# Second layer's down projection by seven products in place of eight

## The chip, the cores and the metric

The kernel runs on one core of a Trainium2 chip. Its engines are TensorE (PE in the profile, with its weight loads as PEld), VectorE (DVE), ScalarE (ACT), GpSimd (POOL) and SyncE (SP, which here issues nearly all DMAs). Each works through its own queue of instructions in order; semaphores order them among each other. On-chip memory is SBUF; PE writes its results to PSUM; DMAs move data between SBUF and the chip's DRAM. The metric is the device time of one execution in microseconds (us), lower is better.

## The reference

One inference step of a two-layer encoder for two request groups: a prompt of 1024 tokens and 8 samples of 16 tokens, 1152 tokens in all, width 1024. Layer 0 mixes tokens with RWKV-7, layer 1 with banded attention, and each ends in a SwiGLU feed-forward with adaptive norms. What matters here is the feed-forward of layer 1 (D_FF = 2816 = 22 x 128):

```python
def swiglu(h, w_gate, w_up, w_down):
    return (jax.nn.silu(h @ w_gate) * (h @ w_up)) @ w_down
...
        h = modulate(rms_norm(x, p['norm_ffn'][l]), sh_f, sc_f)
        x = x + gt_f[:, None, :] * swiglu(h, p['w_gate'][l], p['w_up'][l], p['w_down'][l])
```

All of it is float32. `x + gt_f * ...` is done in the method `residual`: one gate for all prompt tokens, one for each sample.

## The kernel before

**Layout.** Features lie on the 128 partitions, tokens along the free axis. The 1152 tokens are two column groups: c = 0 with 512 prompt tokens, c = 1 with 512 prompt and 128 sample tokens. Each group has two halves, 256 + 256 and 320 + 320.

**Precision.** A float32 product is made of three matmuls (`mm3`, line 143 issues each): both operands are split into a high part `hi` (rounded by ACT, line 272) and the rest `lo` (DVE subtracts, line 273), and hi x hi, hi x lo, lo x hi are added up in PSUM.

**Gate stage** (`gate_up`, called once per 128 rows f of D_FF, 22 of them for a layer). The two matrices `w_gate` and `w_up` are already combined by Winograd's form of Strassen's scheme: seven products instead of eight, each of 4 k x 3 passes x 2 column groups = 24 matmuls. `strassen_weights` loads four raw weight tiles (`rq`, five buffers), makes the combinations on POOL (lines 1340 to 1343) and splits them into the buffers `w`, 16 of them, two per product. The activation's seven combinations are held for the whole stage in the pools h0 and h1 (`slot`, 14 slots for each c). `gate_up` moves the products out of PSUM with ACT and DVE, adds on DVE and POOL (line 1369) and multiplies (lines 1383, 1385) into two tiles s0 and s1, the two token halves. They go to DRAM, to `sd`, by four stores. The first block, f = 0, runs in two calls, one for each c.

**Down stage** (`ffn` from the definition of `begin` on). D_FF is taken in 11 pairs p of two blocks. For each (p, c) the activations come back from `sd`, are split, and for each of the 8 output blocks n the product of this pair is added to an accumulator in SBUF (ACT copies for p = 0, line 1434; DVE adds, line 1436). For c = 0 a matmul has 512 columns, for c = 1 two matmuls have 320 each. For p = 7 the residual is added to the accumulator; for p = 8 to 10 `residual` multiplies by the gate and adds (line 1170, and lines 1174 and 1175 for the samples), and after p = 10 the block is stored.

PSUM tiles of this stage are three (`wide`: one of tag PT, two of tag S), used in turn. Temporary tiles of the gate stage (`ev("t")`) share eleven buffers.

**Order.** The program is written with a tile framework: it derives waits from the tiles, gives buffers out of pools, and orders the instructions of each engine with a simulation of times at build. Within an engine the order is then fixed. `tc.issue_after(ins)` puts what is traced in its block behind `ins` on that engine.

## Time and profile before

| | us |
|---|---|
| median of 3 runs (lowest, highest) | 3810.54 (3801.19, 3811.68) |
| the profiled execution | 3804.49 |
| its span | 3802.7 |
| second layer's down stage, first to last matmul (3520.20 to 3798.80) | 278.6 |
| from there to the end of the span | 3.9 |

The profiled execution lasts 1.8 us longer than the span, which runs from the first recorded instruction to the last. How to read the rows: a group of instructions is written as line, engine, operation, tile written <- tiles read, shape, count, then busy us, mean ns of one, and the engine's idle time just before with what ended it. A row of the timeline has the start, the length, the engine, the line, and in brackets an idle time before it. A row of the chain of waits has the start, the length and what ran. In the table of windows each stretch has the busy time of every engine; PEclk is the share of full speed that the clock was granted.

### The profile page before, as it was taken

Reading aid. Unit: us, or ns where it says so; the run is one execution under the profiler, and the core shown is the slowest. Engines: PE = TensorE matmul, PEld = TensorE weight load, DVE = VectorE, ACT = ScalarE, POOL = GpSimd, SP = SyncE. Lnnn points to the kernel's source line nnn. Section 1 sums busy time; section 2 is a strip of 40 time slices with the busy share of each in tenths; the row PEclk is TensorE's granted clock in tenths of the full one; section 3 lists DMA queues with packets and bytes.
Section 4 is the critical chain, followed back from the end, with each engine's and each line's share of the span. In section 5 each row is a group of like instructions: output and inputs, shape, how many; then the busy total and the mean of one; then the engine's idle time right before and its main releaser. Section 6 shows DMA issues by size and latency. Waiting matters only on the chain.

```text
span 3802.7 us, 72100 instructions
## 1 busy us (share of the span) xinstructions
PE 3506.1 (92%) x28550; PEld 3098.0 (81%) x28550; DVE 2263.6 (60%) x4396; ACT 1573.8 (41%) x3006; POOL 591.6 (16%) x497
## 2 busy tenths in 40 slices
PE   5889989989999799999999899789889799999999
PEld 4777778777667699999888879667677799999898
DVE  4666667765445854554457742666565755545667
ACT  5545546544223533333311452556554533333310
POOL 0000000000011154453000100000000255444000
PEclk9887899899699899999999999899899899999999
DMA  5876776776665322224654122554565322222521
GB/s 212 236 216 170 207 220 184 201 203 201 192 197 176 113 84 76 76 73 157 221 177 172 64 71 92 153 151 155 152 203 178 120 78 71 76 75 96 171 86 66
DMA packets 426995, 554.01 MB, mean 146 GB/s; under 512 B 128385, under 2 KB 292737, under 8 KB 422177
## 3 DMA queue, kind: packets, MB, share of 16 engines
q1 hardware_dynamic: 351344, 450.68, 36.9%
q0 software_dynamic: 22224, 80.36, 6.9%
q10 hardware_dynamic: 53088, 18.36, 2.1%
q8 instruction: 225, 3.69, 0.4%
q14 instruction: 114, 0.93, 0.1%
HBM read 415.85 MB, written 133.40 MB: 144 GB/s over the span
## 4 chain that ended last, share of the span: by engine, by line
PE 69%; DMA 11%; DVE 10%; issue 4%; ACT 4%; SPq 1%; ACTq 0%; POOL 0%; DVEq 0%; POOLq 0%
PE S L143 32%; PE PT L143 15%; PE acc L143 12%; PE st L143 3%; PE O L143 2%; PE G L143 1%; DVE h L273 1%; PE aux L143 1%; PE PT L1811 1%; PE Y L143 1%; DMA TT<-Z 1%; DMA h<-out_kT 1%; DVE wlo L273 1%; DMA raw<-in_rw_o 1%; DMA h<-in_wo 1%
## 5 line engine op out<-in xcount | busy, mean ns | idle before, releaser
L143 PE MATMUL S<-h,w 128*128 128x320 f32 (+1 forms) x4944 | 689.7, 298 | 12.3 <-ACT h L272 4.8
L143 PEld LDWEIGHTS S<-h,w 128*128 128x128 f32 x4944 | 671.8, 191 | 18.4 <-ACT h L272 5.6
L143 PE MATMUL S<-h,wh 128*128 128x320 f32 (+1 forms) x2844 | 529.8, 338 | 15.9 <-DVE h L1170 6.8
L143 PE MATMUL acc<-mx,whi 128*128 128x384 f32 x1728 | 508.5, 372 | 32.7 <-ACT whi L272 13.0
L143 PEld LDWEIGHTS S<-h,wh 128*128 128x128 f32 x2844 | 456.1, 189 | 70.8 <-issue 12.3
L272 ACT ACTIVATE w<-rq 128x512 fp32r<-128x512 f32 x308 | 192.6, 629 | 515.1 <-PE S L143 201.1
L143 PEld LDWEIGHTS acc<-mx,whi 128*128 128x128 f32 x1728 | 337.6, 204 | 63.3 <-ACT whi L272 16.9
L273 DVE TENSOR_TENSOR w<-rq,w 128x512 fp32r<-128x512 f32 x308 | 267.8, 872 | 199.8 <-ACT w L272 199.0
L143 PE MATMUL PT<-h,w 128*128 128x320 f32 (+1 forms) x2448 | 347.6, 297 | 10.2 <-ACT h L272 4.7
L143 PEld LDWEIGHTS PT<-h,w 128*128 128x128 f32 x2448 | 332.1, 190 | 12.2 <-ACT h L272 5.1
L143 PE MATMUL acc<-mx,wlo 128*128 128x384 f32 x864 | 316.1, 366 | 8.3 <-DVE wlo L273 8.3
L1369 POOL TENSOR_TENSOR t<-t,t 128x576 f32<-128x576 f32 (+1 forms) x132 | 226.5, 1717 | 442.2 <-ACT t L1376 320.1
L143 PE MATMUL PT<-h,wh 128*128 128x320 f32 (+1 forms) x1428 | 284.2, 342 | 8.2 <-ACT h L1558 2.3
L143 PEld LDWEIGHTS PT<-h,wh 128*128 128x128 f32 x1428 | 231.7, 188 | 38.5 <-issue 5.0
L143 PEld LDWEIGHTS acc<-mx,wlo 128*128 128x128 f32 x864 | 175.0, 203 | 20.6 <-DVE wlo L273 12.9
L273 DVE TENSOR_TENSOR wlo<-raw,whi 128x1024 fp32r<-128x1024 f32 x114 | 139.1, 1221 | 84.9 <-ACT whi L272 83.8
L272 ACT ACTIVATE wh<-rq 128x512 fp32r<-128x512 f32 x124 | 74.8, 625 | 245.1 <-PE S L143 161.4
L273 DVE TENSOR_TENSOR h<-h,h 128x1024 fp32r<-128x1024 f32 (+4 forms) x112 | 122.3, 1106 | 88.3 <-ACT h L272 72.1
L272 ACT ACTIVATE whi<-raw 128x1024 fp32r<-128x1024 f32 x114 | 119.6, 1053 | 129.0 <-PE acc L143 62.6
L272 ACT ACTIVATE h<-h 128x1024 fp32r<-128x1024 f32 (+4 forms) x112 | 103.5, 935 | 159.8 <-DMA h<-sd 111.1
L1369 DVE TENSOR_TENSOR t<-S,t 128x576 f32<-128x576 f32 (+1 forms) x116 | 86.4, 744 | 122.7 <-PE S L143 122.7
L1436 DVE TENSOR_TENSOR h<-h,S 128x640 f32<-128x640 f32 (+1 forms) x150 | 111.9, 750 | 78.9 <-PE S L143 78.7
(444 smaller groups left out, 5625.0 us busy)
## 6 DMA issues: line engine op xcount, KB each, us to landing
h<-in_wada SPq DMA_DIRECT2D x64, 512.0 KB, 6.3
rq<-in_wg SPq DMA_DIRECT2D x88, 256.0 KB, 2.6
rq<-in_wu SPq DMA_DIRECT2D x88, 256.0 KB, 2.6
rq<-in_wd SPq DMA_DIRECT2D x88, 256.0 KB, 3.1
raw<-in_wada POOLq DMA_DIRECT2D x32, 512.0 KB, 5.0
kc<-in_ck SPq DMA_DIRECT2D x16, 1024.0 KB, 5.1
vc<-in_cv SPq DMA_DIRECT2D x16, 1024.0 KB, 6.0
sd<-t SPq DMA_DIRECT2D x88, 160.0 KB, 1.9
```

What stands on the lines that cost most here:

```text
L143: return nc.tensor.matmul(out, lhsT, rhs, start=start, stop=stop)
L272: self.nc.scalar.activation(hi, x, AF.Copy)
L273: self.nc.vector.tensor_tensor(lo, x, hi, ALU.subtract)
L1369: eng.tensor_tensor(out, x, y, ALU.add)
L1436: nc.vector.tensor_tensor(y, y, d, ALU.add)
L1811: nc.tensor.transpose(pt[:, j * 128:(j + 1) * 128], P[:, j * 128:(j + 1) * 128], self.C("ident"))
```

## The change

The down projection of the second layer is computed by the same kind of seven products. Its three dimensions are halved: D_FF into even and odd blocks f, the 1024 outputs into two halves h of four blocks m, the tokens of each group into their two halves.

- The host stores `w_down[1]` as `wd1`, four quarter matrices side by side in 128 x 4 x 5632.
- During the gate stage of layer 1 `down_sums` makes the four combinations of the weights, in 32 groups g of 176 columns: a load into `ws` (two buffers), four POOL adds behind the last addition of the gate call (`last_add`), a store to the DRAM tiles `Ws`. One or two groups follow each of the calls f = 1 to 21.
- `down_open` returns what takes the place of the four stores: after an even f one block goes to DRAM and its two halves are held; after the odd f that follows, four DVE operations make the combinations and twelve stores write the other six blocks. They are stored by product and column group, as `Bd[c][i]`, each in three tiles of 4, 4 and 3 blocks. The first even block, done in two calls, takes a way through DRAM.
- `down` runs the seven products in the order 0, 1, 2, 4, 5, 6, 3. Each loads and splits its operand (6 loads, 11 k) and, for each of the four m, three pieces of weights, and issues 11 k x 3 passes x 2 column groups. Products 0, 2 and 4 are copied to SBUF and kept (`T`); the others are added to what is kept, and products 1, 5, 6 and 3 finish one quarter of the outputs each: residual and store.
- The buffers `w` are 14 instead of 16 in the second layer.

The first layer's feed-forward keeps the old loop. The diff, cut:

```diff
     for l in range(2):
         d[f"wg{l}"] = _tiles(i["w_gate"][l])
         d[f"wu{l}"] = _tiles(i["w_up"][l])
-        d[f"wd{l}"] = i["w_down"][l].reshape(22, 128, 1024)
+    d["wd0"] = i["w_down"][0].reshape(22, 128, 1024)
+    d["wd1"] = i["w_down"][1].reshape(11, 2, 128, 2, 4, 128).transpose(2, 3, 1, 4, 0, 5).reshape(128, 4, 5632)
     return {k: np.ascontiguousarray(v) for k, v in d.items()}
...
     def wq_open(self, ctx, name):
         self.wq = ctx.enter_context(self.tc.tile_pool(name="wq" + name, bufs=1, reuse_waits="tile"))
-        self.hw = ("w", "w", 16)
+        self.hw = ("w", "w", 14 if name == "1" else 16)
         self.halfraw = lambda: self.wq.tile([128, 512], F32, tag="rq", name=self.nm("rq"), bufs=5)

     def wide_open(self, ctx, name):
...
         yield put(a21)
         yield put(a22)

-    def gate_up(self, sd, B, W, cs):
+    def gate_up(self, put, B, W, cs):

         nc = self.nc
         dve = nc.vector
...
             return t[:, n0:n1]

         def add(eng, out, x, y):
-            eng.tensor_tensor(out, x, y, ALU.add)
+            return eng.tensor_tensor(out, x, y, ALU.add)

         t1, s0, s1, t5, u2, u3 = (new() for _ in range(6))
         nc.scalar.activation(t1, product(0), AF.Copy)
...
         add(gp, s1, s1, u2)
         self.silu = nc.scalar.activation(s1, s1, AF.Silu)
         add(dve, u3, product(6), u2)
-        add(gp, t5, t5, u3)
+        self.last_add = add(gp, t5, t5, u3)
         dve.tensor_tensor(s1, s1, t5, ALU.mult)
         add(dve, u3, product(3), u3)
         dve.tensor_tensor(s0, s0, u3, ALU.mult)
-        for h, s in enumerate((s0, s1)):
-            for c in cs:
-                o, n = 256 * c - n0, (256, 320)[c]
-                t0 = 512 * c + n * h
-                nc.sync.dma_start(sd[:, t0:t0 + n], s[:, o:o + n])
+        put(s0, s1, cs)

     def ffn(self, l, B, W, part1, xsrc, dst, done):

         nc = self.nc
         sd = [self.dp.tile([128, 2, 1152], F32, name=f"sd{l}_{p}") for p in range(11)]
-        self.gate_up(sd[0][:, 0], B, iter(W), (0,))
+
+        def spill(f):
+            def put(s0, s1, cs):
+                for h, s in enumerate((s0, s1)):
+                    for c in cs:
+                        o, n = 256 * (c - cs[0]), (256, 320)[c]
+                        t0 = 512 * c + n * h
+                        nc.sync.dma_start(sd[f // 2][:, f % 2, t0:t0 + n], s[:, o:o + n])
+            return put
+        if l:
+            spill = self.down_open()
+        self.gate_up(spill(0), B, iter(W), (0,))
         for _ in part1:
             pass
-        self.gate_up(sd[0][:, 0], B, iter(W), (1,))
+        self.gate_up(spill(0), B, iter(W), (1,))
         for f in range(1, 22):
-            self.gate_up(sd[f // 2][:, f % 2], B, self.strassen_weights(l, f, nc.vector if f == 1 else None), (0, 1))
+            self.gate_up(spill(f), B, self.strassen_weights(l, f, nc.vector if f == 1 else None), (0, 1))
+            if l:
+                for g in range(32 * (f - 1) // 21, 32 * f // 21):
+                    self.down_sums(g)
+        if l:
+            return self.down(48 * l + 40, xsrc, dst)
         self.ada = self.ada_steps(range(12, 28), "acc", 1) if l == 0 else iter(())
         gate = 48 * l + 40
         acc, end = {}, iter(())
...
                     end = done(c, acc[c], st)
         return end

+    def down_open(self):
+
+        nc = self.nc
+        part = (slice(0, 256), slice(256, 576))
+        self.Bd = [[[self.dp.tile([128, n, (256, 320)[c]], F32, name=f"bd{c}_{i}_{j}") for j, n in enumerate((4, 4, 3))] for i in range(7)]
+                   for c in range(2)]
+        self.Ws = [self.dp.tile([128, 4, 1408], F32, name=f"ws{m}") for m in range(4)]
+        b12 = self.dp.tile([128, 576], F32, name="b12")
+        held = []
+
+        def put(p, i, t):
+            for c in range(2):
+                nc.sync.dma_start(self.Bd[c][i][p // 4][:, p % 4], t[:, part[c]])
+
+        def first(s0, s1, cs):
+            c, = cs
+            nc.sync.dma_start(self.Bd[c][0][0][:, 0], s0)
+            nc.sync.dma_start(b12[:, part[c]], s1)
+
+        def even(p):
+            def f(s0, s1, cs):
+                put(p, 0, s0)
+                held[:] = s0, s1
+            return f
+
+        def odd(p):
+            def f(s0, s1, cs):
+                if p == 0:
+                    held[:] = (self.ev("t")[:, 0:576] for _ in range(2))
+                    for c in range(2):
+                        nc.sync.dma_start(held[0][:, part[c]], self.Bd[c][0][0][:, 0])
+                    nc.sync.dma_start(held[1], b12)
+                e0, e1 = held
+                t6, t3 = (self.ev("t")[:, 0:576] for _ in range(2))
+                put(p, 2, s1)
+                nc.vector.tensor_tensor(t6, s1, e1, ALU.subtract)
+                put(p, 6, t6)
+                nc.vector.tensor_tensor(e1, e1, e0, ALU.subtract)
+                put(p, 4, e1)
+                nc.vector.tensor_tensor(e0, e0, t6, ALU.add)
+                put(p, 5, e0)
+                put(p, 1, s0)
+                nc.vector.tensor_tensor(t3, s0, e0, ALU.subtract)
+                put(p, 3, t3)
+            return f
+        return lambda f: first if f == 0 else (odd if f % 2 else even)(f // 2)
+
+    def down_sums(self, g):
+
+        nc, gp = self.nc, self.nc.gpsimd
+        m, j = divmod(g, 8)
+        q = self.wq.tile([128, 4, 176], F32, tag="ws", name=self.nm("ws"), bufs=2)
+        nc.sync.dma_start(q, self.a["wd1"][:, :, g * 176:(g + 1) * 176])
+        with self.tc.issue_after(self.last_add.ins):
+            gp.tensor_tensor(q[:, 3], q[:, 2], q[:, 3], ALU.add)
+            gp.tensor_tensor(q[:, 2], q[:, 0], q[:, 2], ALU.subtract)
+            gp.tensor_tensor(q[:, 0], q[:, 3], q[:, 0], ALU.subtract)
+            gp.tensor_tensor(q[:, 1], q[:, 1], q[:, 0], ALU.subtract)
+        nc.sync.dma_start(self.Ws[m][:, :, j * 176:(j + 1) * 176], q)
+
+    def down(self, gate, xsrc, dst):
+
+        nc = self.nc
+        ks = [(j, k) for j, n in enumerate((4, 4, 3)) for k in range(n)]
+        part = (slice(0, 256), slice(256, 576))
+        T = {}
+
+        def operand(i):
+            X = {0: [], 1: []}
+            for c in range(2):
+                n = (256, 320)[c]
+                for j, nk in enumerate((4, 4, 3)):
+                    raw, hi, lo = (self.slot(c, dt)[:, :nk * n].rearrange("p (k t) -> p k t", k=nk) for dt in (F32, F32R, F32R))
+                    nc.sync.dma_start(raw, self.Bd[c][i][j])
+                    self.split(hi, lo, raw)
+                    X[c].append((hi, lo))
+            return X
+
+        def weights(i, m):
+            src = {0: 0, 1: 1, 3: 3}.get(i)
+            src = self.Ws[m][:, {5: 0, 2: 1, 6: 2, 4: 3}[i]] if src is None else self.a["wd1"][:, src, m * 1408:(m + 1) * 1408]
+            W = []
+            for o, n in ((0, 512), (512, 512), (1024, 384)):
+                raw = self.halfraw()[:, :n]
+                nc.sync.dma_start(raw, src[:, o:o + n])
+                W.append([self.wq.tile([128, 512], F32R, tag="w", name=self.nm("w"), bufs=self.hw[2]) for _ in range(2)])
+                self.split(W[-1][0][:, :n], W[-1][1][:, :n], raw)
+            return W
+
+        def hold(n):
+            T[n] = [self.slot(c)[:, :4 * (256, 320)[c]].rearrange("p (m t) -> p m t", m=4) for c in range(2)]
+
+        def result(h, t, m, o):
+            f = 4 * h + m
+            at = [slice(512 * c + (256, 320)[c] * t, 512 * c + (256, 320)[c] * (t + 1)) for c in range(2)]
+            x = self.ev("xin")[:, 0:576]
+            for c in range(2):
+                nc.sync.dma_start(x[:, part[c]], xsrc[:, f, at[c]])
+            self.residual(448 if t else 576, f, gate, o, x, o)
+            for c in range(2):
+                nc.sync.dma_start(dst[:, f, at[c]], o[:, part[c]])
+
+        for i in (0, 1, 2, 4, 5, 6, 3):
+            X = operand(i)
+            if i in (0, 2, 4):
+                hold(i)
+            for m in range(4):
+                W = weights(i, m)
+                d = self.wide()[:, 256:832]
+                for c in range(2):
+                    for n, (j, k) in enumerate(ks):
+                        s = slice(k * 128, (k + 1) * 128)
+                        hi, lo = (X[c][j][h][:, k] for h in range(2))
+                        self.mm3(d[:, part[c]], W[j][0][:, s], W[j][1][:, s], hi, lo, n == 0, n == 10)
+                z = [d[:, part[c]] for c in range(2)]
+                t = {n: [T[n][c][:, m] for c in range(2)] for n in T}
+                o = None if i in (0, 2, 4) else self.ev("o")[:, 0:576]
+
+                def add(out, a, b):
+                    for c in range(2):
+                        nc.vector.tensor_tensor(out[c], a[c], b[c], ALU.add)
+                if i in (0, 2, 4):
+                    for c in range(2):
+                        nc.scalar.activation(t[i][c], z[c], AF.Copy)
+                oc = None if o is None else [o[:, part[c]] for c in range(2)]
+                if i == 1:
+                    add(oc, z, t[0])
+                    result(0, 0, m, o)
+                elif i == 4:
+                    add(t[2], t[2], t[4])
+                elif i == 5:
+                    add(t[0], z, t[0])
+                    add(oc, t[2], t[0])
+                    result(0, 1, m, o)
+                elif i == 6:
+                    add(t[0], z, t[0])
+                    add(oc, t[4], t[0])
+                    result(1, 1, m, o)
+                elif i == 3:
+                    add(oc, z, t[0])
+                    result(1, 0, m, o)
+
     def dense(self, x2, x3, close):
         nc = self.nc
         self.kT, self.x2, self.x3 = self.o["kT"], x2, x3
```

More of the change, by code (lines that the diff above doesn't have):

```diff
@@ L1327, in put @@
         def put(t):
-            hi, lo = (self.wq.tile([128, 512], F32R, tag="w", name=self.nm("w"), bufs=16) for _ in range(2))
+            hi, lo = (self.wq.tile([128, 512], F32R, tag="w", name=self.nm("w"), bufs=self.hw[2]) for _ in range(2))
             self.split(hi, lo, t)
@@ L1489, in weights @@
                         yield
-                for _ in part(0, lambda: self.wq.tile([128, 512], F32, tag="w", name=self.nm("x"), bufs=16)):
+                for _ in part(0, lambda: self.wq.tile([128, 512], F32, tag="w", name=self.nm("x"), bufs=self.hw[2])):
                     pass
```

## The prediction

> **What bounds the kernel now.** I read the page's totals first, then the engines' busy time in the stages of the second feed-forward layer (the table of windows), then the chain of waits there, and the timeline for the shapes.
>
> ```profile
> span 3802.7 us, 72100 instructions
> ...
> PE 3506.1 (92%) x28550; PEld 3098.0 (81%) x28550; DVE 2263.6 (60%) x4396; ACT 1573.8 (41%) x3006; POOL 591.6 (16%) x497
> ```
> ```profile
> 3100.00:3500.00 400.00, 400.00 (x3008) 400.00 (x3007) 204.54 (x234) 128.65 (x215) 192.53 (x124) 1.00 0.22 75
> 3520.20:3798.80 278.60, 277.48 (x1587) 253.19 (x1585) 190.31 (x299) 54.19 (x73) 0.00 (x0) 1.00 0.32 105
> 3798.80:3802.70 3.90, 0.01 (x1) 0.00 (x0) 0.75 (x1) 0.00 (x0) 0.00 (x0) 1.00 0.34 134
> ```
>
> The windows' columns are length, PE, PEld, DVE, ACT, POOL, granted clock, DMA share and GB/s. The first row lies inside the gate stage, the second is the whole down projection, the third the tail. PE is busy all the time in the first two at a granted clock of 1.00, and no other engine comes near. A busy PE need not be PE at its peak, so the next question is its pace. From the chain of waits:
>
> ```profile
> 3491.78 3.19 PE PT L143 x24
> 3494.97 6.39 PE S L143 x48
> ...
> 3520.51 1.39 PE PT L143 x6
> ...
> 3771.74 3.52 PE S L143 x24
> ...
> 3781.13 2.72 PE S L143 x12
> ...
> 3797.45 1.37 PE S L143 x6
> ```
>
> and the timeline's shapes of the same stretches:
>
> ```profile
> 3491.61 3.36 PE L143 MATMUL PT<-h,w 128*128 128x256 f32 x24
> 3738.15 1.92 PE L143 MATMUL PT<-h,wh 128*128 128x320 f32 x12
> 3780.97 2.88 PE L143 MATMUL S<-h,wh 128*128 128x512 f32 x12
> ```
>
> The chain is PE behind PE. A matmul of 512 columns takes 2.72/12 = 226.7 ns, one of 320 takes 3.52/24 = 146.7 ns, and the gates' half-and-half mixture of 256 and 320 (the timeline merges both under the first shape) takes 6.39/48 = 133.1 ns. All three lie on 13 ns + 0.417 ns per column. So both stages are bound by the number of columns PE streams plus 13 ns a matmul.
>
> **The change, part by part.**
>
> *Matmuls removed and added.* The old loop issues per f (22) and n (8) three 512-column and six 320-column matmuls: 22 x 8 x (3 x 226.7 + 6 x 146.7) = 274.6 us. The stage lasts 278.6, so 4.0 us are gaps. The new one has 7 products x 4 m x 11 k x 3 passes x (256 and 320) = 1848 matmuls. That is the gates' mixture: 1848 x 133.1 = 246.0 us, 8.78 us for each of 28 blocks. **Gain 28.6 us**; the columns fall by 1/8 but there are 264 matmuls more at 13 ns.
>
> *Gaps.* I keep the 4.0 us: ends 0 and 43 (the first rival). *Tail.* The last block ends in an add per column group, the residual, and the store; before, in one residual and the store. The added work on the path:
>
> ```profile
> L1436 DVE TENSOR_TENSOR h<-h,S 128x640 f32<-128x640 f32 x37 | 30.2, 819 | 17.3 <-PE S L143 17.3
> L1436 DVE TENSOR_TENSOR h<-h,S 128x512 f32<-128x512 f32 x38 | 25.4, 682 | 8.4 <-PE S L143 8.4
> L273 DVE TENSOR_TENSOR wh<-rq,wh 128x512 fp32r<-128x512 f32 x37 | 24.1, 684 | 2.4 <-ACT wh L272 2.4
> L1170 DVE SCALAR_TENSOR_TENSOR h<-S,mod,h 128x512 f32<-128x512 f32 x32 | 23.9, 750 | 14.4 <-PE S L143 14.3
> L273 DVE TENSOR_TENSOR h<-h,h 128x1280 fp32r<-128x1280 f32 x10 | 14.9, 1491 | 6.1 <-PE S L143 3.2 <-PE PT L143 1.6 <-ACT h L272 1.3
> ...
> L1174 DVE TENSOR_TENSOR xin<-S,mod 128x128 f32<-128x128 f32 x16 | 4.5, 280 | 0.0
> ```
> ```profile
> L272 ACT ACTIVATE wh<-rq 128x512 fp32r<-128x512 f32 x37 | 21.6, 625 | 100.5 <-PE S L143 67.5 <-issue 19.4 <-PE PT L143 13.7
> L272 ACT ACTIVATE h<-h 128x1280 fp32r<-128x1280 f32 x10 | 12.7, 1275 | 23.0 <-DMA h<-sd 18.6 <-DVE h L1436 3.9 <-DVE h L273 0.5
> ```
>
> By the two L1436 rows an add costs 1.07 ns a column over 135 ns: 0.48 us for 320. **Minus 0.5 us.**
>
> *DVE and ACT inside the new stage.* Per 8.78 us block DVE splits three weight halves (3 x 0.68), a quarter of the next operand (6336/4 columns at 1.491/1280 = 1.85 us) and, in the worst products (indices 5 and 6), four adds (1.77) and the residual (0.75 and two of 0.28): 7.0 us at most. It fits, with 20% left. ACT: 3 x 0.63 + 1.6 = 3.5 us. Neither reaches the path: a weight tile is split over one block ahead (14 buffers, 6 per block), and a PSUM tile is reused only three blocks later.
>
> *Operands of the next product.* These need slots of the pools h0/h1, 14 each. The running product holds 6 (hi and lo of three tiles), kept results at most 3, so 5 are free: raw, hi and lo of the first tile, again for the second, the third's raw; its hi and lo come free when the last m has passed its first four k. PE needs that third tile eight k into the next product. So loading is covered by the 35 us of the running product. The wait that moves closest: product 1 reads the odd f's first half, written after the last gate; product 0, which needs none of f = 21, covers that.
>
> *Gate stage.* One gate_up call takes 7 x 24 x 133.1 ns = 22.36 us. It gets 32/21 = 1.5 (1 or 2) groups of four POOL adds, and every second call four DVE adds of 576.
>
> ```profile
> L1369 POOL TENSOR_TENSOR t<-t,t 128x576 f32<-128x576 f32 x54 | 90.4, 1674 | 179.5 <-ACT t L1376 127.3 <-DVE t L1369 50.9 <-DMA rq<-in_wu 1.4
> L1343 POOL TENSOR_TENSOR rq<-rq,rq 128x512 f32<-128x512 f32 x18 | 23.2, 1288 | 12.3 <-DMA sd<-t 8.9 <-POOL rq L1342 3.4
> ```
> ```profile
> L1383 DVE TENSOR_TENSOR t<-t,t 128x576 f32<-128x576 f32 x18 | 31.9, 1773 | 23.7 <-POOL t L1369 23.7
> L1385 DVE TENSOR_TENSOR t<-t,t 128x576 f32<-128x576 f32 x18 | 13.4, 744 | 0.0
> ```
> ```profile
> 3294.66 1.86 POOL L1369 TENSOR_TENSOR t<-t,t 128x576 f32<-128x576 f32 x1 [1.39 <-DMA rq<-in_wu]
> 3302.60 1.29 POOL L1343 TENSOR_TENSOR rq<-rq,rq 128x512 f32<-128x512 f32 x1 [0.68 <-DMA sd<-t]
> 3310.96 1.42 POOL L1369 TENSOR_TENSOR t<-t,t 128x576 f32<-128x576 f32 x1 [7.07 <-ACT t L1376]
> ```
>
> No POOL add of 176 columns is shown. Bounds: 0.44 us (1.288 x 176/512) and 1.29 (as dear as 512); I take 0.6, nearer the low one, since 512 columns cost 1.29. POOL is busy 192.5 us in 400/22.36 = 17.9 calls, 10.8 per call; a two-group call comes to 15.6, by the upper bound 21.1, below 22.36. The new adds stand after the last addition (3296.5), and what is queued behind them is the next weights' four sums, then the next call's first add at 3310.96; idle there is 7.1 us, and two groups take 4.8. The sums may come 5 us later. ACT, which waits for them, is seven weight pairs (7 x 3.19 us = 22) ahead of PE now (16 buffers are eight pairs, one in use), and six with 14 (19 us), so PE keeps 14 us. If that cover were gone, each call would lose what the sums are late: up to 5 us.
>
> DVE: 204.5/17.9 = 11.4 us per call. Four adds more in odd calls are 3.0 us (0.744 each) to 7.1 (1.773 each, the row of the add that stands beside POOL), 1.5 to 3.5 on average, and POOL's adds can hold DVE back by their own length, 3.7 to 7.9. Average 16.6 to 22.8 of 22.36: the low end hides, the upper would just overflow; I take 0 on the path. This is one place where a page warns: the Trainium skill, "GPSIMD Engine Reference", section "1. Specifications", says that GpSimd shares its SBUF interface with VectorE and contends with DVE instructions of two SBUF inputs. The trace agrees (L1383 1.773 us, L1385 0.744); taken at full length it gives the upper figure above.
>
> *SP and DMA.* Per call SP issues 8 DMAs now; it gets 7 stores on average in place of 4 (12 in odd calls), and 3 for the sums. What is queued behind a store that waits is the next raw weights, which today land like this:
>
> ```profile
> SPq L1335 <- DVE w L273: 193.4, 68, 3.6
> ```
> ```profile
> L1335 SPq DMA_DIRECT2D rq<-in_wg x40: 327/333/333, 3055.2 to 3464.4; - x40
> ```
> ```profile
> rq<-in_wg SPq DMA_DIRECT2D x34, 256.0 KB, 2.5
> ```
> ```profile
> GB/s 212 236 216 170 207 220 184 201 203 201 192 197 176 113 84 76 76 73 157 221 177 172 64 71 92 153 151 155 152 203 178 120 78 71 76 75 96 171 86 66
> ```
>
> SP spends its time waiting for free buffers (the first row, us in total, times, longest), not issuing (0.33 us each): 14 issues are 5 us of 22.36. Bytes, from the tiles' sizes: 23 MB for the sums and 10 more for operands in 470 us, 70 GB/s beside the 75 of the gate window; the page's second slice ran at 236. In the down stage 43 MB in 250 us is 172 GB/s. I take 0; the ends are 0 and the 14 us that PE is covered for, once.
>
> *Fewer weight buffers at the start.* f = 0 keeps all 14 until its second half runs. f = 1's first split waits today for its DMA and not for a buffer, so I take 0:
>
> ```profile
> 3034.79 0.63 ACT L272 ACTIVATE w<-rq 128x512 fp32r<-128x512 f32 x1 [2.02 <-DMA rq<-in_wg]
> ```
>
> **Sum:** -28.6 + 0.5 = -28.1 us. The profiled execution took 3804.49, so 3776.4. The three runs' median, 3810.54, lies 6.05 above it and gives 3782.4; I forecast the middle, **3779**, 0.8% faster.
>
> **The rivals.**
>
> (1) *Slower: operands that can't be loaded ahead.* At each of the six switches PE waits for a load (4.4 us by the row below), ACT's split (1.28) and DVE's (1.49): 7.2 us, 43 in all, so 3779 + 43 = 3822.
>
> ```profile
> h<-sd SPq DMA_DIRECT2D x10, 640.0 KB, 4.4
> ```
> It decides once fewer than three slots are free while a product runs, or a DMA on SP stands in front of the loads until the product ends. Against: the count of five free slots. Only at the three switches where two or three results are held, it is 21.6: 3801. Chances 0.08 and 0.07.
>
> (2) *DVE overflows in the gate stage* by the upper average, 0.5 us x 21 = 10.5 us: 3789.5. For: the 1.773 us row; against: half of DVE's time is idle now. Chance 0.08.
>
> (3) *The change doesn't do what it says:* smaller matmuls are no cheaper per product, because the weight load sets the pace. If the mixture cost 146.7 like the 320s, the stage would be 1848 x 146.7 = 271 us, 25 above the forecast's, and the time 3804: no change. The gates' 133.1 ns, same shapes and same 128-column weights, speaks against. The Trainium skill, "TensorE: Matmul & The Clock Gate", section "Back-to-back issue gap", gives a sustained spacing of about 81 ns at 128 columns and 131 at 512, so a much larger fixed part; the trace disagrees (226.7 ns at 512). Chance 0.01.
>
> The forecast keeps 0.76. **Range:** from 3769 (the runs' lowest, 3801.19, less 28.1 and less the 4.0 of gaps) to 3794 (the highest, 3811.68, less 28.1, with rival 2's 10.5); left out are rivals 1 and 3, 0.16. Faster by over 0.3% (11.4 us, about what a measurement of this kernel can tell): forecast and rival 2, 0.84, less a little for unknown sides, 0.82; within 0.3%: 0.10; slower: 0.08.
>
> **What would show it.** In the profile after: 28 blocks of 66 matmuls, 8.78 us each; a down stage near 250 us from first matmul to last; PE at 50 of 50 us in the gate windows with POOL near 14 us a call. A wait of PE for ACT or DVE on an h tile at switches is rival 1; idle PE in odd calls rival 2; 66 matmuls over 9.5 us rival 3. Wrong altogether it would be if stages before the second feed-forward layer moved, which I hold fixed.

## The result, and the profile after

| | us |
|---|---|
| kernel before, median of 5 runs (lowest, highest) | 3802.37 (3801.19, 3811.68) |
| changed kernel, median of 5 runs | 3789.1 (3784.2, 3792.12) |
| ratio | 0.995, 95% interval 0.9935 to 0.9966 |
| the changed kernel's profiled execution, its span | 3791.94, 3790.1 |

The changed kernel is 0.5% faster. The forecast was 3779 in a range of 3769 to 3794, so the time lies in the range, but the gain is 13 us where 28 were worked out. A second measurement, below among the experiments, gave 0.9942 (0.9928 to 0.9955) with 29 runs of the kernel before. One execution of experiment 6 was slow, at 6389.87 us against at most 3794.81 of its other five, and its ratio leaves it out.

First the totals of the changed kernel's page, then its table of windows: the same 400 us inside the gate stage, the down stage from its first matmul to its last, and the tail (columns: length, PE, PEld, DVE, ACT, POOL, granted clock, DMA share, GB/s).

```profile
span 3790.1 us, 73177 instructions
...
PE 3479.0 (92%) x28814; PEld 3094.8 (82%) x28814; DVE 2244.3 (59%) x4348; ACT 1611.3 (43%) x3074; POOL 687.2 (18%) x625
```
```profile
3100.00:3500.00 400.00, 400.00 (x3008) 400.00 (x3007) 234.58 (x270) 130.49 (x216) 278.87 (x234) 1.00 0.44 143
3537.90:3785.20 247.30, 246.59 (x1849) 246.12 (x1848) 135.98 (x211) 89.93 (x142) 10.32 (x9) 1.00 0.61 201
3785.20:3790.10 4.90, 0.00 (x0) 0.00 (x0) 1.63 (x3) 0.00 (x0) 0.00 (x0) 1.00 0.17 60
```

PE's 3008 matmuls in 400 us are the same number as before although POOL's busy time grew from 192.53 to 278.87 us: the gate stage costs PE nothing. The down stage fell from 278.6 to 247.3 us, and PE is busy in 246.6 of them. The changed kernel's chain of waits (start, length, what ran) shows how even it is:

```profile
3541.79 6.07 PE PT L144 x41
3547.85 17.47 PE S L144 x131
3565.32 8.79 PE PT L144 x66
3574.11 17.59 PE S L144 x132
...
3776.36 8.80 PE PT L144 x66
...
3785.19 0.07 DVE o L1587
...
3785.53 0.49 DVE o L1587
...
3786.05 0.82 DVE o L1171
```

A block of 66 matmuls takes 8.79 us, two of them 17.59, and after the first block nothing but PE stands on the chain. No product switch shows a wait.

So where are the missing microseconds? The timeline has the first gate weight load of layer 1, issued just before the second feed-forward layer begins, for the kernel before and for the changed one:

```profile
3002.77 0.87 SPq L1335 DMA_DIRECT2D rq<-in_wg  x2
```
```profile
3020.05 0.87 SPq L1336 DMA_DIRECT2D rq<-in_wg  x2
```

From there to the end of the span it is 3802.7 - 3002.77 = 799.9 us before and 3790.1 - 3020.05 = 770.1 after: the layer gained **29.9 us**. But it began 17.3 us later, after work that the change doesn't touch. The view of the tile `rq` shows that most of this is there by the first such load of layer 0 (the numbers on both sides of "to" are the first and the last start):

```profile
L1335 SPq DMA_DIRECT2D rq<-in_wg x88: 327/333/452, 1234.1 to 3464.4; - x88
```
```profile
L1336 SPq DMA_DIRECT2D rq<-in_wg x88: 327/333/850, 1248.7 to 3485.1; - x88
```

Layer 0's token mixing, with the same instructions in the same order on every engine, lasted 1234.1 us in one profiled execution and 1248.7 in the other (the time up to that load).

### The profile page after: what moved, and what is told of

The parts are those of the page before. It is cut to its first block, busy times and chain, and to the rows that moved or that the text cites. A ratio compares the mean times of both kernels' runs of the same rounds, so it can differ in the third digit from the quotient of the medians.

```text
span 3790.1 us, 73177 instructions
## 1 busy us (share of the span) xinstructions
PE 3479.0 (92%) x28814; PEld 3094.8 (82%) x28814; DVE 2244.3 (59%) x4348; ACT 1611.3 (43%) x3074; POOL 687.2 (18%) x625
## 4 chain that ended last, share of the span: by engine, by line
PE 69%; DMA 11%; DVE 10%; issue 5%; ACT 4%; SPq 1%; ACTq 0%; POOL 0%; DVEq 0%; POOLq 0%
PE S L144 31%; PE PT L144 15%; PE acc L144 13%; PE st L144 3%; PE O L144 2%; PE G L144 2%; DVE h L274 1%; PE aux L144 1%; DMA raw<-in_rw_o 1%; PE PT L1966 1%; DMA h<-out_kT 1%; PE Y L144 1%; DMA bt<-in_rel 1%; DMA TT<-Z 1%; DVE wlo L274 1%
## 5 line engine op out<-in xcount | busy, mean ns | idle before, releaser
L144 PE MATMUL S<-h,w 128*128 128x256 f32 (+1 forms) x6132 | 849.8, 298 | 13.0 <-ACT h L273 5.5
L144 PEld LDWEIGHTS S<-h,w 128*128 128x128 f32 x6132 | 830.8, 191 | 19.0 <-ACT h L273 6.3
L273 ACT ACTIVATE w<-rq 128x512 fp32r<-128x512 f32 (+1 forms) x392 | 240.8, 620 | 574.7 <-PE S L144 241.5
L144 PE MATMUL PT<-h,w 128*128 128x256 f32 (+1 forms) x3108 | 437.8, 297 | 9.6 <-ACT h L273 4.2
L274 DVE TENSOR_TENSOR w<-rq,w 128x512 fp32r<-128x512 f32 (+1 forms) x392 | 318.7, 817 | 214.5 <-ACT w L273 194.8
L144 PE MATMUL S<-h,wh 128*128 128x320 f32 (+1 forms) x1794 | 336.7, 338 | 14.8 <-DVE h L1171 5.9
L144 PEld LDWEIGHTS S<-h,wh 128*128 128x128 f32 x1794 | 286.6, 190 | 54.7 <-issue 11.9
L274 DVE TENSOR_TENSOR h<-h,h 128x1024 fp32r<-128x1024 f32 (+5 forms) x132 | 145.6, 1117 | 108.6 <-ACT h L273 95.7
L273 ACT ACTIVATE h<-h 128x1024 fp32r<-128x1024 f32 (+6 forms) x132 | 123.1, 944 | 160.6 <-DMA h<-bd 56.3
L273 ACT ACTIVATE whi<-raw 128x1024 fp32r<-128x1024 f32 x114 | 119.7, 1054 | 135.1 <-PE acc L144 76.1
L144 PE MATMUL acc<-h,wh 128*128 128x256 f32 (+1 forms) x864 | 137.7, 308 | 18.1 <-ACT wh L273 9.9
```

What stands on the lines that cost most here:

```text
L144: return nc.tensor.matmul(out, lhsT, rhs, start=start, stop=stop)
L273: self.nc.scalar.activation(hi, x, AF.Copy)
L274: self.nc.vector.tensor_tensor(lo, x, hi, ALU.subtract)
```

## The experiments

In what follows "the layer" is the second feed-forward layer, from its first gate weight load (of layer 1) to the end of the span: 799.9 us in the kernel before, 770.1 in the changed one.

**1. Does the first stage vary by itself, or does the change move it?** Four kernels ran on one chip, together with 29 runs of the kernel before. Two are copies.

> The kernel before, unchanged. The second feed-forward layer's gain in the traces is about 30 us, the medians differ by 13, and the first gate weight load stands at 1234.1 us before and at 1248.7 after although the work up to there is the same on every engine. Theory A (the change moves something of the program, such as where its inputs, scratch tensors or code lie, and that slows layer 0): the first gate weight load again within 3 us of 1234, and the time near 3802. Theory B (that stage varies from execution to execution): the load anywhere between 1225 and 1255, and the time by as much above or below 3802.

> The changed kernel, unchanged. Theory A: the first gate weight load again within 3 us of 1249, the time near 3789. Theory B: the load anywhere between 1225 and 1255, and the time follows it. By both the down stage lasts 247 us from its first matmul to its last.

The third has the inputs in another order, the fourth a larger scratch:

```diff
-        d[f"wd{l}"] = i["w_down"][l].reshape(22, 128, 1024)
+    for l in range(2):
+        d[f"wd{l}"] = i["w_down"][l].reshape(22, 128, 1024)
```

> The kernel before with its two down projection inputs declared behind all the others, in the order that the changed kernel has. No instruction differs. Theory A, if the inputs' order is what counts: the first gate weight load near 1249 and the time 13 to 16 us above the kernel before's. Theory B, or A by another cause: no difference beyond the spread of the copy of the kernel before.

```diff
                         nc.sync.dma_start(dst[:, n, self.cols(c)], y)
+                        if l and n == c == 0:
+                            pad = self.dp.tile([128, 42112], F32, name="pad")
+                            nc.sync.dma_start(pad[:, 0:9], y[:, 0:9])
```

> The kernel before with one more scratch tensor of 21.6 MB in DRAM, behind all others, so that the scratch is as large as the changed kernel's (one small store into it in the last stage is the only instruction added). Theory A, if the size of the scratch is what counts: the first gate weight load near 1249 and the time 13 to 16 us above the kernel before's. Theory B, or A by another cause: no difference beyond the spread of the copy of the kernel before.

| | median us (lowest, highest) | ratio to before, 95% | first gate load | the layer |
|---|---|---|---|---|
| kernel before, 29 runs | 3808.29 (3795.95, 3825.22) | | 1234.1 (first profile) | 799.9 |
| copy of before | 3809.83 (3800.0, 3818.4) | 1.0002 (0.9987 to 1.0016) | 1251.6 | 798.9 |
| inputs reordered | 3809.81 (3798.86, 3821.1) | 1.0006 (0.9992 to 1.0019) | 1235.4 | 799.0 |
| larger scratch | 3809.16 (3793.04, 3820.05) | 1.0003 (0.9985 to 1.0021) | 1238.4 | 799.4 |
| copy of the changed kernel | 3784.58 (3778.93, 3789.09) | 0.9942 (0.9928 to 0.9955) | 1243.2 | 770.3 |

The copy of the kernel before shows most of the answer. Its rows, from the view of the tile and from the table of windows (columns as above), the latter beside the first profile's:

```profile
L1335 SPq DMA_DIRECT2D rq<-in_wg x88: 327/333/453, 1251.6 to 3475.5; - x88
```
```profile
0.00:1234.00 1234.00, 1082.64 (x11300) 885.67 (x11300) 755.33 (x1659) 596.92 (x1146) 86.22 (x168) 0.87 0.68 201
```
```profile
0.00:1251.60 1251.60, 1092.96 (x11300) 894.70 (x11300) 755.64 (x1659) 598.47 (x1146) 86.21 (x168) 0.86 0.68 198
```

The same program took 17.5 us longer for the same 11300 matmuls, with PE busy 10.3 us longer at a clock granted at 0.86 in place of 0.87. The traces' record of the granted clock has two values only, 1.00 and 0.50, and the mean says how long each held: in this stage 0.50 held for 318 us in the first profile and for 345 in the copy's. Over all 14 profiles on record, the later experiments included, a longer stage goes with more time at 0.50 (from 301 to 375 us; correlation 0.90). Which of the two drives the other isn't shown.

So the spread that theory B speaks of is there: this stage varies from execution to execution, by as much as the two first profiles differ. The order of the inputs and the size of the scratch, theory A's two candidates, don't make the 13 to 16 us that were expected of them; a shift of about 5 us these intervals can't exclude. The layer varies by 1.0 us among the four profiles with the old down stage. And the five runs of before that stood in the first result were low, by chance or by their chip, which isn't on record: the 29 have their median 5.9 us higher.

Not everything is settled by it. By these profiles the layer gains 28.6 to 29.9 us, and the medians differ by 23.7, with an interval of 17.1 to 27.4 (0.9955 and 0.9928 of 3808.29). Between 1 and 13 us are lost in stages with the same instructions.

All the profiles and medians on record together say that this isn't spread alone. The nine profiles of kernels with the new down stage (the first, the copy here, and those of experiments 2 to 4 and 6) have their first gate load at 1243.2 to 1258.3 us and begin the layer at 3011.8 to 3024.0; of the four with the old one three lie below, at 1234.1 to 1238.4 and at 3000.0 to 3003.2, and only the copy, at 1251.6 and 3014.1, does not. Taking the layer (799.3 us, the mean of four, for the old one) and the 1.8 us outside the span off a median leaves what the stages before the layer took: 3007.2 us for the 29 runs of before and 3012.5 for the copy of the changed kernel. In each run of experiments 2 to 4 and 6 the stages before the layer also come out longer than in the runs of before of the same measurement, by 3 to 10 us. No run shows why. Experiment 5 comes back to that.

**2. How much room has POOL in the gate stage?** The sums' four additions become eight, then twelve, each time by undoing and redoing one:

```diff
             gp.tensor_tensor(q[:, 3], q[:, 2], q[:, 3], ALU.add)
+            gp.tensor_tensor(q[:, 3], q[:, 3], q[:, 2], ALU.subtract)
+            gp.tensor_tensor(q[:, 3], q[:, 2], q[:, 3], ALU.add)
...
             gp.tensor_tensor(q[:, 1], q[:, 1], q[:, 0], ALU.subtract)
+            gp.tensor_tensor(q[:, 1], q[:, 1], q[:, 0], ALU.add)
+            gp.tensor_tensor(q[:, 1], q[:, 1], q[:, 0], ALU.subtract)
```

> The changed kernel with every group's four POOL additions made eight (two are undone and made again). At the 0.78 us that such an addition takes in the changed kernel's trace POOL is busy 10.8 + 12.2 x 0.78 = 20.3 us of a gate call's 22.36, and 23.3 in a call with two groups. If PE's lead over the gate weights covers what they are late, as the prediction has it: no change, gate stage 469.5 us, time within 3 us of the changed kernel's. If the sums have no cover: the calls with two groups lose 0.9 us or more each, 10 us and up.

> The changed kernel with every group's four POOL additions made twelve. POOL then needs 10.8 + 18.3 x 0.78 = 25.1 us a call, 2.7 more than the call lasts. POOL becomes the bound: 21 x 2.7 = 57 us longer, less up to 14 us that the weights' lead hides, so 43 to 57. If VectorE beside POOL slows the additions, or POOL slows VectorE's splits, more than that; if POOL's additions are much cheaper without waits, less.

The table of windows over the same 400 us, with eight additions and then with twelve:

```profile
3100.00:3500.00 400.00, 400.00 (x3007) 400.00 (x3007) 256.48 (x268) 127.88 (x213) 350.41 (x341) 1.00 0.44 143
```
```profile
3100.00:3500.00 400.00, 364.90 (x2639) 357.63 (x2638) 226.49 (x235) 108.55 (x187) 332.47 (x390) 0.98 0.39 121
```

With eight, POOL is busy 350.41/17.9 = 19.6 us of a call's 22.36, and PE doesn't lose one: the layer is 769.0 us, the median 3784.73 (ratio 0.9923, 0.99 to 0.9947). So there is cover, as the prediction claimed. With twelve the cover is gone: the layer is 835.8 us, **65.7 longer**, the median 3851.9 (1.0105, 1.0084 to 1.0126). Expected were 43 to 57. The waits of this kernel in the same stretch (what waited for what: us in total, times, longest) say where the rest went:

```profile
ACT t L1381 <- POOL t L1370: 94.8, 15, 7.0
ACT w L273 <- POOL rq L1344: 90.2, 16, 9.1
```
```profile
POOL ws L1521 <- DMA ws<-in_wd: 28.6, 11, 3.5
```

ACT waits for the sums of the gate weights and for the gate's own additions, both queued behind the extra work. And POOL itself idles 28.6 us for the next group's load; that the two `ws` buffers are held longer is the likely reason, but no run had more of them.

The expectation's reason was wrong: POOL was to become the bound, with 25.1 us of work a call. A call now lasts 22.36 x 3008/2639 = 25.5 us, and POOL is busy for 332.47 of the 400, which is 21.2 us of a call and less than the 22.36 that PE needs; the sums' additions took 0.66 us on average in place of 0.78. On average over the stage no engine is full, PE included (364.90 of 400). The time goes into waits of the engines for one another, which a sum of busy times doesn't show.

**3. What if the operands can't be loaded ahead?** The first attempt occupied five slots of each pool with a memset at the start and one in the last product:

```diff
+            if i == 0:
+                kept = [self.slot(c) for c in range(2) for _ in range(5)]
+                for k in kept:
+                    nc.vector.memset(k[:, 0:1], 0.0)
...
+                    if m == 0:
+                        for k in kept:
+                            nc.vector.memset(k[:, 0:1], 0.0)
```

> The changed kernel with five of the fourteen slots of each h pool kept occupied during the down stage, so that at most two are free while a product runs: this is the prediction's first rival made true. By its price, six switches of 7.2 us (a load, ACT's split, VectorE's split): 43 us longer, PE waiting at each switch for a split of an h tile. If slots that come free inside the running product's last block are enough, less: 0 to 15 us.

The layer was 770.6 us and the median 3787.91 (0.9933, 0.991 to 0.9956), but this says nothing of the rival. In this kernel's timeline both memsets stand at the beginning of the down stage:

```profile
3536.97 0.07 DVE L1576 MEMSET h<- 128x1 f32 x2
...
3543.06 0.08 DVE L1614 MEMSET h<- 128x1 f32 x3
```

The second (line 1614) depends on nothing that is computed late, so it was ordered right behind the first and the slots were free again. In the next attempt the last use is an addition that needs the last product's result, and four slots are kept:

```diff
-                            nc.vector.memset(k[:, 0:1], 0.0)
+                            nc.vector.tensor_tensor(k[:, 0:1], o[:, 0:1], k[:, 0:1], ALU.add)
```

> The changed kernel with four of the fourteen slots of each h pool kept to the last product by an addition into them that needs its result. Free slots while a product runs: 3, 3, 2, 1, 1, 2 at the six switches. The prediction's first rival decides at fewer than three free slots: four switches of 7.2 us, 29 us longer than the changed kernel. The other theory: a slot that PE leaves inside the product's last block is early enough, since the first column group's first tile is done some 7 us before the block ends, and its split takes about 2.3 us: 0 to 8 us longer.

Now the additions stand in the last product (first row), and this kernel's waits of PE in the down stage are the two rows after it:

```profile
3761.55 0.63 DVE L1613 TENSOR_TENSOR h<-o,h 128x1 f32<-128x1 f32 x8
```
```profile
PE PT L144 <- DVE h L1576: 1.1, 1, 1.1
PE S L144 <- ACT h L273: 0.2, 1, 0.2
```

The layer took 3789.0 - 3017.70 = 771.3 us, 1.2 more than in the changed kernel, and the median was 3790.6 (0.9944, 0.9927 to 0.9961). The wait of 1.1 us is one at the stage's start that the changed kernel has too (0.7 us there). All six switches together cost 0.2 us, not 29: the second theory's 0 to 8 holds. The chain suggests how: around the switches the order built for PE mixes short runs of one product's last block with the next product's first,

```profile
3645.47 1.08 PE S L144 x9
3646.55 4.49 PE PT L144 x32
3651.04 0.96 PE S L144 x8
...
3652.15 0.96 PE S L144 x8
3653.11 1.18 PE PT L144 x8
```

which the changed kernel's even blocks of 66 don't. As I read it, a late operand tile delays the matmuls that need it, while the others go first. So this is an answer for a PE order that was built for the scarce slots.

**4. Is a matmul of fewer columns cheaper?** The third rival said that the weight load sets the pace. The first column group is cut in halves:

```diff
-                for c in range(2):
+                for c, p in ((0, slice(0, 128)), (0, slice(128, 256)), (1, slice(0, 320))):
```

(and `[:, p]` on the operand and on the PSUM tile).

> The changed kernel with the 256 columns of the first column group multiplied in two halves of 128: 924 matmuls of 256 columns become 1848 of 128. By the prediction's law, 13 ns and 0.417 ns a column, 924 x 119.7 ns = 110.6 us become 1848 x 66.3 = 122.6: 12 us longer. If a matmul of few columns is no cheaper (the third rival, that the weight load or something else sets the pace), each half costs as much as the whole: 111 us longer.

The chain of this kernel, and the window of its second row:

```profile
3579.60 24.41 PE S L144 x198
3604.01 12.21 PE PT L144 x99
```
```profile
3604.00:3616.20 12.20, 12.20 (x102) 12.20 (x101) 3.49 (x6) 1.78 (x4) 0.00 (x0) 1.00 0.36 108
```

A block has 66 matmuls of 128 columns and 33 of 320. The latter are 33 x 146.7 ns = 4.84 us, which leaves 7.37/66 = 111.7 ns for one of 128 columns, where one of 256 takes (8.79 - 4.84)/33 = 119.7. Half the columns, 7% less time. The layer became 95 us longer (864.9), which is neither the 12 of the law nor quite the 111 of the rival; the median 3879.3 (1.0183, 1.0156 to 1.0209). To see whether this is a floor, five products got five cuts:

```diff
+                cut = {1: (256, 160), 2: (256, 80), 4: (128, 320), 5: (64, 320), 6: (32, 320)}.get(i, (256, 320))
+                for c, p in [(c, slice(u, u + cut[c])) for c in range(2) for u in range(0, (256, 320)[c], cut[c])]:
```

> The changed kernel with the columns cut in five of the seven products: 320 in halves of 160 (product 1), 320 in quarters of 80 (2), 256 in halves of 128 (4), in quarters of 64 (5), in eighths of 32 (6). By the law of 13 ns and 0.417 ns a column a block of 8.79 us becomes 9.2, 10.1, 9.2, 10.1, 11.8. If instead every matmul lasts at least the 111.6 ns that the halves of 128 took: 11.3, 18.7, 12.2, 19.6, 34.3, and the time 208 us longer than the changed kernel's.

The chain has blocks of product 1 (99 matmuls), 2 (165), 5 (x330 are two blocks) and 6 (x594 are two); the windows lie inside the same blocks (length, PE's busy time, granted clock, DMA share, GB/s):

```profile
3593.38 11.31 PE PT L144 x99
...
3643.00 29.30 PE PT L144 x165
...
3788.02 61.69 PE S L144 x330
...
4030.27 117.25 PE S L144 x594
```
```profile
3593.40:3604.60 11.20, 11.20 (x100) 1.00 0.51 165
...
3643.00:3672.20 29.20, 29.20 (x166) 0.62 0.39 137
...
3788.00:3818.80 30.80, 30.80 (x168) 0.61 0.30 101
...
4030.30:4147.40 117.10, 117.10 (x594) 0.56 0.07 21
```

At 160 columns the floor holds to the digit: 11.31 us, expected 11.3 (and product 4, halves of 128 again, took 12.21). At 80, 64 and 32 the blocks take 29.3, 30.8 and 58.6 us, more than the floor's 18.7, 19.6 and 34.3; there the clock fell to 0.62, 0.61 and 0.56. Times the clock they are 18.2, 18.8 and 32.8, the floor again within 5%. So the law of 13 ns and 0.417 ns a column ends between 256 and 160 columns, at a floor of about 112 ns (the two meet at an estimated 237 columns).

The clocks above are means over blocks that mix two widths; inside a block it is a step. In the trace of product 2's first block the matmuls of 80 columns begin at about 3620, the clock reads 1.00 up to 3625, and from 3625.4 to 3642.9 it reads 0.50, with PE busy all the time; in the next block, which begins with 256 columns, it is 1.00 again from 3646. At 0.50 the trace has 79 matmuls of 80 columns in 16.5 us and 119 of 32 columns in 25 us, 209 and 210 ns each. The floor is the same for both and nearly doubles as the clock halves, so it is for the most part not a fixed time from outside PE's clock.

The Trainium skill, "TensorE: Matmul & The Clock Gate", section "LDWEIGHTS (loading the stationary operand)", puts a weight load, in nanoseconds, at its columns divided by 1.2; for the 128 here that gives an estimate of 107 ns, near the floor that the runs show. That the weight load is the floor's cause is argued from this; no run changed the weights' width. The layer as a whole took 1171.4 us, 401 more than in the changed kernel where the floor at full clock gave 208; the two runs took 4179.55 and 4189.4.

**5. The gate part alone.** The old spills are kept beside the new stores, and the old down loop follows, its steps in plain order:

```diff
+            old, new = spill, self.down_open()
+
+            def spill(f):
+                a, b = old(f), new(f)
+
+                def put(s0, s1, cs):
+                    a(s0, s1, cs)
+                    b(s0, s1, cs)
+                return put
...
-        if l:
-            return self.down(48 * l + 40, xsrc, dst)
```

> The changed kernel's gate stage (operands and weights' sums written as well as the old spills) followed by the down projection of the kernel before, in the plain order of its steps. If the gate part costs nothing, as the prediction has it: the second feed-forward layer within 5 us of the kernel before's, whatever is lost at switches of its weight buffers included, and the median within 5 us of 3809. If the larger program is what lengthens the stages before that layer by the 6 us by which the medians fall short of the traces' 30: the layer as before, and the median near 3815.

```profile
3100.00:3500.00 400.00, 400.00 (x3008) 400.00 (x3008) 232.94 (x269) 129.66 (x215) 276.95 (x233) 1.00 0.52 170
```

The table of windows shows PE full in the gate stage even with both sets of stores: the gate part costs nothing there. The layer took 3805.3 - 3002.46 = 802.8 us, 2.9 more than before. The median is 3815.63, near the 3815 of the second expectation and 6.5 above before's 3809.14 of that measurement (1.0014, 1.0002 to 1.0025, or 0.8 to 9.5 us). Taking the 2.9 off leaves 3.6 for the stages before, with an interval of -2.1 to 6.6. That decides for neither expectation: the larger program may lengthen the early stages by some microseconds or not at all. In its profile the first gate load stands at 1236.6, like three of the four profiles of the old down stage. This stays open.

**6. A shorter tail.**

```diff
+                nc.vector.scalar_tensor_tensor(x[:, part[c]], t0[c], g, x[:, part[c]], ALU.mult, ALU.add)
+            o = self.ev("o")[:, 0:576]
+            for c in range(2):
+                nc.vector.scalar_tensor_tensor(o[:, part[c]], z[c], g, x[:, part[c]], ALU.mult, ALU.add)
```

> The changed kernel with the last product's result taken in one step for each column group: the gate times the held sum is added to the residual input before the product ends, so that after the last matmul VectorE has one operation of 320 columns left instead of an addition of 320 and one of 576. From the last matmul to the end 4.94 us become about 4.1, 0.8 less; the median differs from the changed kernel's by less than its runs spread.

From its table of windows:

```profile
3789.30:3793.00 3.70, 0.00 (x0) 0.00 (x0) 0.94 (x2) 0.00 (x0) 0.00 (x0) 1.00 0.22 80
```

The tail is 3.7 us instead of 4.9, a little better than expected: the timelines have the stores issued 0.5 us after the last matmul, where the changed kernel (the second row) had them 1.7 us after it.

```profile
3789.84 0.81 SPq L1581 DMA_DIRECT2D out_y<-o  x2
```
```profile
3786.89 0.81 SPq L1567 DMA_DIRECT2D out_y<-o  x2
```

The ratio, 0.9946 (0.9929 to 0.9962), is that of the changed kernel within either interval: 1.2 us can be read from the trace (the layer took 769.0), not from the times.

## Why the prediction was right, and where it was not

**Matmuls: right.** 1848 matmuls in 28 blocks, predicted at 8.78 us each, took 8.79. The pace from the gates' mixture carried over. That is the cause of the gain: 28.5 of the layer's 29.9 us.

**Gaps: mis-sized.** I kept the old 4.0 us; measured are 247.3 less 28 blocks of 8.79, 246.1, so 1.2. That is 2.8 us of gain not counted.

**Tail: mis-sized.** I took 0.5 us more and it was 1.0 (4.9 against 3.9): an addition of 0.49 for the second column group alone, then a residual over all 576 columns, 0.82. Experiment 6 took 1.2 back. Together -28.5 - 2.8 + 1.0 = -30.3; the other 0.4 lies ahead of the stage, whose first matmul comes 517.9 us after the first gate weight load and not 517.4.

**Gate stage: right, by terms that were partly wrong.** DMA moved 143 GB/s in the 400 us, where 75 + 70 were reckoned; in the down stage it moved 201 and not 172. PE stayed busy in both. POOL came to 278.87/17.9 = 15.6 us a call, not 14. The new additions took 0.70 to 0.85 us, above the 0.6 that I took and inside its bounds:

```profile
L1522 POOL TENSOR_TENSOR ws<-ws 128x176 f32<-128x176 f32 x27 | 22.5, 847 | 0.7
...
L1524 POOL TENSOR_TENSOR ws<-ws 128x176 f32<-128x176 f32 x27 | 18.5, 697 | 0.7
```

DVE came to 234.58/17.9 = 13.1 us a call, below even the low end of 16.6 to 22.8. I had let POOL's additions hold DVE back by their own length. Experiment 2 prices that: about 107 more additions of POOL in the same 400 us raised DVE's busy time from 234.58 to 256.48 us, 0.2 us for each. The add that stood beside POOL even got shorter in the changed kernel:

```profile
L1384 DVE TENSOR_TENSOR t<-t,t 128x576 f32<-128x576 f32 x18 | 19.9, 1105 | 22.4 <-POOL t L1370 22.4
```

1.105 us against 1.773 before, while the new ones of line 1504 took 1.842. In the call whose line 1504 starts at 3318.42 it runs beside two of POOL's sums of gate weights: the contention seems to move to whatever stands beside POOL. The page that the prediction drew on ("GPSIMD Engine Reference", section "1. Specifications", of the Trainium skill) is borne out in that there is contention. The prediction's own step, to charge every addition at its full length, was far too dear. So rival 2, the overflow of DVE, was not near.

**PE's cover: right.** Doubling the sums cost nothing, and only with twelve additions did PE stop.

**Operands: right, for a reason that wasn't needed.** No switch waited. But the prediction's point of decision, fewer than three free slots, is wrong: with one or two free at four switches PE lost 0.2 us (experiment 3), where the rival had 7.2 a switch. It priced a load and two splits as if PE had nothing else to do at a switch. Experiment 3 shows this for four of 14 slots kept, not for none free.

**Fewer buffers at the start: right.** From the first gate weight load to the first matmul of f = 1 it was 3050.86 - 3002.77 = 48.1 us before, and after:

```profile
3068.33 0.86 PE L144 MATMUL PT<-h,w 128*128 128x256 f32 x5
```

3068.33 - 3020.05 = 48.3.

**Rival 3: rightly set aside, with a wrong law behind it.** At 256 and 320 columns the pace was as forecast, but 256 is only 8 ns above a floor that I hadn't seen (experiment 4).

**What failed** is what the last sentence of the prediction holds fixed, the stages before the second feed-forward layer; by its own words the prediction was wrong there, though its time lay in the range. The layer gained 29.9 us where 28.1 were worked out. The forecast then put this gain on times of before that spread over 10 us in three runs, and on one profile whose first stage, at 1234.1 us, was short. A copy of the same kernel shows that stage at 1251.6 us, and the same program has medians of 3802.37 and 3808.29. The changed kernel's first profile had the stage at 1248.7, and that is most of the 17.3 us between the layer's gain and the difference of the two profiled executions. Beyond this spread the stages ahead of the layer took 3 to 10 us longer, by the medians of the changed kernel and its variants, with the same instructions, and the cause stays open. That 3789.1 us still lay in the range was luck in part: the range reached to 3794 only by the highest run of before and the 10.5 us of rival 2, a cost that no run showed.

## What to carry to other kernels

A gain worked out for one stage should be checked in that stage, from a landmark that both traces have; here a stage that the change didn't touch moved by 17 us between two executions of one program. Halving the columns of a matmul paid only down to a floor of about 112 ns, reached below 256 columns, so count the matmuls as well as the columns before dividing further. To learn whether an engine off the path has room, double its suspected work and see if the bound engine notices; that gave a plain answer where adding up durations did not (13.1 us a call for VectorE against 16.6 to 22.8).

## What the runs showed of the hardware

- A matmul with a weight load of 128 columns of its own took 226.7, 146.7 and 119.7 ns at 512, 320 and 256 columns, and 112 ns at 160 and at 128.
- In stretches of 80, 64 and 32 columns the granted clock fell from 1.00 to 0.50, in the block read closely about 5 us after they began, although PE was busy in every window; over whole blocks that is 0.56 to 0.62. In stretches of 160 and of 128 columns, some 7.4 us long and so longer than those 5, it stayed at 1.00. By 0.417 ns a column against the floor of 112 ns, an estimate from the rows above, columns stream 30% of the time in a stretch of 80 columns and 48% in one of 128, so the clock seems to follow the streaming and not the busy time.
- At the clock of 0.50 a matmul of 80 or of 32 columns took 209 to 210 ns, about twice the floor.
- When POOL's additions of 176 columns were doubled, VectorE's busy time rose by 0.2 us for each, not by their length of 0.7 to 0.85.
- Layer 0's token mixing, the same instructions each time, took 1234.1 to 1258.3 us in 14 profiles, and longer with more time at a granted clock of 0.50.
